# A hybrid encoder layer on one core: the MLP as seven products of 512x512x512 per block instead of eight, with its tokens in two groups of 1024

## The chip, the core and the metric

The kernel runs on one core of a Trainium2 chip. The metric is the device time of one execution in microseconds (us); lower is better. The core has TensorE (PE, matrix products into PSUM; PEld is its weight load), VectorE (DVE), ScalarE (ACT) and GpSimd (POOL) for element work, and SyncE (SP), which here issues most of the transfers; POOL issues the stores, too. Each engine runs its own instructions in order and waits on semaphores for the others. Transfers run on 16 DMA engines.

## The reference

One layer over 2048 tokens of width 1024, in float32: a projection to six parts, two kinds of mixing, an output projection, and a squared-ReLU MLP.

```python
h = rms_norm(x, norm_mix);  proj = h @ w_in                    # [2048,1024] @ [1024,3072]
na_q, na_k, na_v, r_q, r_k, r_v, r_g = split(proj)
na_out = neighbourhood_attention(na_q, na_k, na_v, rpb)        # 8 heads of 64, 32 rows x 64 columns of tokens
ret = bidirectional_retention(rotary(r_q), rotary(r_k), r_v)   # 4 heads, 16 chunks of 128, a scan over chunks
ret_out = silu(r_g) * head_group_norm(ret)
x = x + concat(na_out, ret_out) @ w_out                        # [2048,1024] @ [1024,1024]
h = rms_norm(x, norm_mlp)
x = x + square(relu(h @ w_up)) @ w_down                        # 1024 -> 4096 -> 1024
return rms_norm(x, norm_final)
```

## The kernel before, in words

**Products.** Every float32 product is three matmuls on operands that are split into a rounded part and a rest (`hi`, `lo`): hi x hi, hi x lo, lo x hi (`mm3`, L187 to L189, each 128x512). A split is one ACT cast (L175 for weights) and one DVE subtraction (L176). Weights stream from DRAM in pieces of 128 x 1024 elements (512 KB) by `ws`, with two raw buffers.

**Steps.** The main line of the program is a list of steps of 12 matmuls each. `interleave(main, fillers)` emits it, and spreads the other work (the fillers, generators with a first and a last step) between these steps. TensorE's order is this program order; what a filler's matmul waits for stops everything behind it. The steps are: projection 0 to 191 (two passes over `w_in`, for token blocks 0, 1 and then 2, 3), the output projection of block 0 192 to 207, then for each of the four blocks of 512 tokens 144 steps: 128 of the MLP (`mlp_up` and `mlp_down` alternating over eight 512-wide blocks of the hidden layer) and 16 of the next block's output projection.

**Fillers.** Neighbourhood attention runs in four groups `na(j)` of 32 tiles: two score matmuls, softmax on ACT and DVE, transposes, the product with the values (`nv`, loaded tile by tile), an add. Retention first makes its 16 chunk products (`kv`) and the `scan`; then `ret(j)` makes four chunks (`ret_chunk`, 26 yields), each with a single buffer `rg`. `na(0)` lies over steps 50 to 179 and `ret(0)` over 155 to 187; the other groups of both lie under the MLP of the block before: `na(j)` over some 107 steps, `ret(j)` over some 81. The tokens of a block stay in SBUF from the output projection to the end (`big` tiles), where the MLP's results are added to them (L979).

One retention chunk (L731 to L800) runs like this: load `rg` (L741); its exponential on ACT (L746); one add and four reciprocals on DVE (L753, L755); their product back into `rg` (L756); scores and outputs on TensorE (`rs`, `ro`, L769 to L776); statistics, the norm and the multiplication by `rg` on DVE (L780 to L789). Only after L789 is `rg` free for the next chunk's load.

## Time and profile before

| | |
|---|---|
| time, median of 3 executions | 2452.12 us (2449.55 to 2459.75) |
| the profiled execution: its span, first to last instruction | 2451.4 us |
| PE / PEld / DVE / ACT / POOL busy | 2410.5 / 1965.4 / 1396.9 / 962.0 / 176.4 us |
| mean granted TensorE clock | 0.995 of full speed |
| moved by DMA | 378.32 MB, 154 GB/s over the span |

The profiled execution is one more execution of the same kernel; its span is 0.7 us under the median of the three that were timed. "Busy" of an engine is the sum of its instructions' durations; matmuls overlap in the pipeline, and their ends are modelled, so what a matmul costs is read from the time between starts.

### The profile page before, as it was taken

Reading aid. Unit: us, or ns where it says so; the run is one execution under the profiler, and the core shown is the slowest. Engines: PE = TensorE matmul, PEld = TensorE weight load, DVE = VectorE, ACT = ScalarE, POOL = GpSimd, SP = SyncE. Lnnn points to the kernel's source line nnn. Section 1 sums busy time; section 2 is a strip of 40 time slices with the busy share of each in tenths; the row PEclk is TensorE's granted clock in tenths of the full one; section 3 lists DMA queues with packets and bytes.
Section 4 is the critical chain, followed back from the end, with each engine's and each line's share of the span. In section 5 each row is a group of like instructions: output and inputs, shape, how many; then the busy total and the mean of one; then the engine's idle time right before and its main releaser. Section 6 shows DMA issues by size and latency. Waiting matters only on the chain.

```text
span 2451.4 us, 31720 instructions
## 1 busy us (share of the span) xinstructions
PE 2410.5 (98%) x11384; PEld 1965.4 (80%) x11384; DVE 1396.9 (57%) x2810; ACT 962.0 (39%) x1690; POOL 176.4 (7%) x266
## 2 busy tenths in 40 slices
PE   7999999999999999999999999999999999999998
PEld 6888788867788887788777878888887888888886
DVE  7325354466467667545766665467666555544445
ACT  6223343323354444424544443345444423423223
POOL 1212022221100000000000000000000000000001
PEclk9999999999999999999999999999999999999999
DMA  8635566776645545543755554447554443433332
GB/s 284 185 120 171 164 200 198 239 249 188 225 136 164 155 144 157 150 134 91 226 164 146 155 156 128 129 126 213 141 156 123 119 137 96 144 101 95 95 101 71
DMA packets 238957, 378.32 MB, mean 154 GB/s; under 512 B 29009, under 2 KB 101329, under 8 KB 238801
## 3 DMA queue, kind: packets, MB, share of 16 engines
q1 hardware_dynamic: 218640, 315.46, 43.8%
q0 software_dynamic: 20160, 60.84, 7.4%
q8 instruction: 90, 1.47, 0.2%
q14 instruction: 67, 0.54, 0.1%
HBM read 313.28 MB, written 62.91 MB: 153 GB/s over the span
## 4 chain that ended last, share of the span: by engine, by line
PE 85%; DMA 6%; DVE 4%; issue 3%; ACT 2%; POOL 1%; SPq 1%; DVEq 0%; POOLq 0%; ACTq 0%
PE mm L187 26%; PE mm L189 25%; PE mm L188 25%; PE op L649 2%; PE sp L609 2%; PE tp L634 2%; DMA mraw<-d_mix 1%; DMA nv<-d_v 1%; PE sp L607 1%; PE rs L769 1%; DMA xT<-in_xT_dram 1%; PE hp L299 1%; PE ro L775 1%; DMA nql<-d_ql 1%; PE ro L776 1%
## 5 line engine op out<-in xcount | busy, mean ns | idle before, releaser
L187 PE MATMUL mm<-wh,big 128*128 128x512 f32 (+1 forms) x1784 | 700.5, 393 | 5.6 <-DVE st L440 4.7
L189 PE MATMUL mm<-wh,big 128*128 128x512 f32 (+1 forms) x1784 | 684.7, 384 | 0.5 <-DVE big L831 0.5
L188 PE MATMUL mm<-wl,big 128*128 128x512 f32 (+1 forms) x1784 | 684.3, 384 | 0.0
L176 DVE TENSOR_TENSOR wl<-raw,wh 128x1024 fp32r<-128x1024 f32 x334 | 410.6, 1229 | 449.8 <-ACT wh L175 441.6
L175 ACT CAST wh<-raw 128x1024 fp32r<-128x1024 f32 x336 | 353.2, 1051 | 720.8 <-PE mm L189 371.3
L187 PE MATMUL mm<-big,wh 128*128 128x512 f32 (+1 forms) x1376 | 545.6, 396 | 2.3 <-DVE st L440 2.3
L189 PE MATMUL mm<-big,wl 128*128 128x512 f32 (+1 forms) x1376 | 530.4, 385 | 0.0
L188 PE MATMUL mm<-big,wh 128*128 128x512 f32 (+1 forms) x1376 | 530.1, 385 | 0.0
L187 PEld LDWEIGHTS mm<-wh,big 128*128 128x128 f32 x1784 | 336.4, 189 | 79.6 <-issue 15.0
L189 PEld LDWEIGHTS mm<-wh,big 128*128 128x128 f32 x1784 | 336.5, 189 | 69.6 <-DVE big L831 1.4
L188 PEld LDWEIGHTS mm<-wl,big 128*128 128x128 f32 x1784 | 337.0, 189 | 59.8
L187 PEld LDWEIGHTS mm<-big,wh 128*128 128x128 f32 x1376 | 258.5, 188 | 61.7 <-issue 12.4
L189 PEld LDWEIGHTS mm<-big,wl 128*128 128x128 f32 x1376 | 258.5, 188 | 53.9
L188 PEld LDWEIGHTS mm<-big,wh 128*128 128x128 f32 x1376 | 259.0, 188 | 45.3
L979 DVE TENSOR_TENSOR big<-mm,big 128x512 f32<-128x512 f32 x248 | 166.6, 689 | 30.5 <-PE mm L189 29.6
L618 ACT ACTIVATE ns<-ns,nsc 128x288 f32<-128x288 f32 (+3 forms) x128 | 79.2, 618 | 230.1 <-DVE nsc L617 229.9
L612 DVE CUSTOM_DVE_ANT_0 ns<-sp,nb 128x288 f32<-128x288 f32 (+3 forms) x128 | 70.8, 553 | 97.4 <-PE sp L609 93.8
L636 ACT CAST npt<-tp 96x384 fp32r<-96x384 f32 (+3 forms) x128 | 64.3, 502 | 119.0 <-PE tp L634 118.9
L637 DVE TENSOR_TENSOR npt<-tp,npt 96x384 fp32r<-96x384 f32 (+3 forms) x128 | 74.7, 584 | 63.2 <-ACT npt L636 63.1
L940 DVE TENSOR_TENSOR st<-mm,st 128x512 f32<-128x512 f32 x128 | 87.3, 687 | 31.4 <-ACT st L939 31.0
L939 ACT ACTIVATE st<-mm 128x512 f32<-128x512 f32 x128 | 75.8, 597 | 62.5 <-PE mm L189 59.5
L620 ACT ACTIVATE ns<-ns,nsc 128x288 f32<-128x288 f32 (+3 forms) x128 | 79.2, 619 | 32.6 <-DVE nsc L619 32.3
(184 smaller groups left out, 1901.2 us busy)
## 6 DMA issues: line engine op xcount, KB each, us to landing
raw<-in_w_up_dram SPq DMA_DIRECT2D x128, 512.0 KB
raw<-in_w_down_dram SPq DMA_DIRECT2D x128, 512.0 KB
raw<-in_w_in_dram SPq DMA_DIRECT2D x48, 512.0 KB
raw<-in_w_out_dram SPq DMA_DIRECT2D x32, 512.0 KB
nv<-d_v SPq DMA_DIRECT2D x288, 36.0 KB
big<-in_x_dram SPq DMA_DIRECT2D x19, 512.0 KB
d_v<-st POOLq DMA_DIRECT2D x32, 256.0 KB, 4.9
nqh<-d_qh SPq DMA_DIRECT2D x64, 128.0 KB
```

The lines of the kernel that those rows point to most:

```text
L175: act.copy(out=hi, in_=t)
L176: (eng or dve).tensor_sub(out=lo, in0=t, in1=hi.bitcast(F32))
L187: pe.matmul(bank, lhsT=sh, rhs=mh, start=first, stop=False)
L188: pe.matmul(bank, lhsT=sh, rhs=ml, start=False, stop=False)
L189: pe.matmul(bank, lhsT=sl, rhs=mh, start=False, stop=last)
L612: dve.tensor_tensor_reduce(out=s, in0=s_ps, in1=btile[t][:, :n], scale=1.0, scalar=-3e38, op0=ALU.add, op1=ALU.max, accum_out=sc[:, 0:1])
L618: act.activation(out=s, in_=s, func=AF.Exp, bias=sc[:, 1:2], scale=1.0, accum_out=sc[:, 2:3])
L620: act.activation(out=s, in_=s, func=AF.Copy, scale=sc[:, 3:4])
L637: dve.tensor_sub(out=pt[:, :, 1], in0=t_ps, in1=pt[:, :, 0].bitcast(F32))
L939: act.activation(out=r, in_=ps, func=AF.Relu)
L940: dve.tensor_tensor(out=r, in0=ps, in1=r, op=ALU.mult)
L979: dve.tensor_tensor(out=sl, in0=ps, in1=sl, op=ALU.add)
```

## The change

The matrix work of the MLP is arranged anew. The first 1024 tokens and the second are one group each. A block of 1024 hidden columns is, for a group, a product of 1024x1024x1024; it was eight products of 512x512x512 and is now seven (Strassen's scheme in Winograd's form), for the up and for the down projection. Each product is four units of 12 matmuls: 7 x 4 x 16 = 448 units for the MLP where there were 512 steps. The scheme needs sums of quarter matrices beforehand and adds of products behind:

- up: the seven left-hand sides `S(i)` of a group's normalised tokens are made once (`prep_first_half`, `prep_rest`), split, stored to DRAM (`d_s`, 2 MB each) and loaded again for each of the four blocks, by POOL as one `wide` tile of 2 MB for each product. The sums of the weights are made on DVE from four raw quarters of 1 MB each (`Weight`).
- down: the weights' side is split to `wide` tiles on ACT and DVE, the activations' side to `narrow` tiles unit by unit; the results are added into eight `y` tiles and a shared `v`.
- The tokens between the output projection and the MLP go through DRAM (`d_y`), as do the normalised, transposed tokens (`d_hT`).
- The weights of the MLP are read twice rather than four times.
- The program falls in two stages with memory of their own. Stage 1 (224 steps): the projection in thirteen pieces (`CHUNKS`) instead of twelve pairs, the output projection of blocks 0 and 1, `na(0)` and `na(1)`, and all of retention: `kv(8, 16)` over 6 steps where it was 15, the scan over 6 where it was 10, and `ret(0)` to `ret(3)` back to back over 15 to 18 steps each. Stage 2 (480 units): 448 of the MLP and, at units 168 to 199, the output projection of blocks 2 and 3. `na(2)` and `na(3)` lie over units 10 to 164.

In the diff `quarter` loads a 128x512 piece of `d_hT`; the first list of products is that of an up block, the second that of a down block. `interleave`, `na`, `kv`, `scan` and `ret_chunk` are as before but for their buffers' pools.

```diff
-    ORDER_A = ["v", "k", "q", "rqk", "rv", "rg"]
-    ORDER_B = ["rqk", "rv", "k", "v", "q", "rg"]
+    CHUNKS = [("v", (0, 1)), ("k", (0, 1, 2)), ("q", (0, 1)), ("v", (2,)), ("rqk", (0, 1)), ("rv", (0, 1)), ("rg", (0, 1)),
+              ("rqk", (2, 3)), ("rv", (2, 3)), ("k", (3,)), ("v", (3,)), ("rg", (2, 3)), ("q", (2, 3))]
...
+    def put(g, i, kk, src):
+        turn2[0] += 1
+        o = np_.tile([P, 2, 512], F32R, tag=("n_k", "n_pt")[turn2[0] % 2], bufs=1, name=nm("so"))
+        act.copy(out=o[:, 0], in_=src)
+        dve.tensor_sub(out=o[:, 1], in0=src, in1=o[:, 0].bitcast(F32))
+        sp.dma_start(out=d_s[g][i][:, kk], in_=o.bitcast(F32))
...
+    def prep_rest(g):
+        for kk in range(4):
+            a11 = quarter(g, 0, kk, "n_qh")
+            a21 = quarter(g, 1, kk, "n_b")
+            a22 = quarter(g, 1, kk + 4, "n_v")
+            a12 = quarter(g, 0, kk + 4, "n_ql")
+            s1 = np_.tile([P, 512], F32, tag="n_t2", bufs=1, name=nm("s1"))
+            dve.tensor_tensor(out=s1, in0=a21, in1=a22, op=ALU.add)
+            dve.tensor_tensor(out=a21, in0=a11, in1=a21, op=ALU.subtract)
+            dve.tensor_tensor(out=a11, in0=s1, in1=a11, op=ALU.subtract)
+            put(g, 5, kk, a11)
+            dve.tensor_tensor(out=a12, in0=a12, in1=a11, op=ALU.subtract)
+            put(g, 6, kk, a21)
+            put(g, 3, kk, a22)
+            put(g, 4, kk, s1)
+            put(g, 2, kk, a12)
+            yield
...
+        def S(i):
+            return [lambda W: st_dma.dma_start(out=W.bitcast(F32), in_=d_s[g][i]), None, None, None]
...
+        return [
+            Product(S(0), T((0, 0)), e1, more=True),
+            Product(S(1), T((1, 0)), e2, joins=True),
+            Product(S(5), [T2(m) for m in range(4)], e6, pre=[lambda: tt(w.t[0, 0], w.t[0, 1], w.t[0, 0], SUB)]),
+            Product(S(6), T((0, 1)), e7, more=True, pre=[lambda: tt(w.t[0, 1], w.t[1, 1], w.t[0, 1], SUB)], then=ld),
...
+        return [
+            Product(T((0, 0)), S((0, 0)), shared(first_block), more=True),
+            Product(T((1, 0)), S((0, 1)), into(0, 0, "2"), joins=True),
+            Product([T3(0), None, T3(1), None], [S3(m) for m in range(4)], into(1, 1), more=True),
+            Product(T((1, 0)), S((1, 1)), into(1, 0), joins=True, then=ld),
+            Product(T((0, 1)), S((0, 0)), shared(None), pre=[sums], then=ld),
+            Product(T((0, 0)), S((1, 0)), into(1, 1, "5"), more=True, then=ld),
+            Product(T((1, 1)), S((0, 1)), into(0, 1, "3"), joins=True, then=ld),
...
-                (unlend(("g", "st", "kT", "qxT")), 1, 134, 134), (scan(), 17, 145, 154),
-                (ret(0), RET_STEPS, 155, 187),
-                (na(0), NA_STEPS, 50, 179),
-            fill.append((ret(j), RET_STEPS, m - 6, m + 75))
+                (unlend(("g", "st", "kT", "qxT")), 1, 150, 150), (scan(), 17, 151, 156),
+                (na(1), NA_STEPS, 112, 183),
+                (ret(0), RET_STEPS, 157, 171), (ret(1), RET_STEPS, 172, 188),
+                (ret(2), RET_STEPS, 189, 204), (ret(3), RET_STEPS, 205, 222),
+                (late(lambda: norm_in(0)), 5, 210, 215), (late(lambda: prep_first_half(0)), 4, 216, 221)]
         interleave(main, fill)
+        first.close()
...
+        fill = [(late(lambda: norm_in(1)), 5, 2, 5), (late(lambda: prep_rest(0)), 4, 6, 6),
+                (late(lambda: na(2)), NA_STEPS, 10, (o0 - 6) // 2), (late(lambda: na(3)), NA_STEPS, (o0 - 6) // 2 + 1, o0 - 4),
...
+        interleave(run_products(prods), fill)
```

Three places show how instructions move. The first is SP's queue between two loads of `rg`, where the weight loads (`raw`) mark how many main steps lie between. Before, inside the MLP of block 0, these are the last rows ahead of the load of `rg_7492` (`nv`, `nk`, `nqh` and `nb` are attention's loads, `rst`, `rqk`, `rqx` and `rv` retention's); the load of `rg` before that one stands sixteen rows above them, with five more weight pieces on the way.

```order
L163 DMA raw_7201<-in_w_down_dram 128x2x512
L574 DMA nk_7211<-d_kl 64x1024
L577 DMA nqh_7214<-d_qh 64x512
L631 DMA nv_7264<-d_v 32x4x128 x2
L163 DMA raw_7262<-in_w_down_dram 128x2x512
L631 DMA nv_7264<-d_v 32x4x128 x2
L737 DMA rqx_7487<-d_rqT 64x4x128 x2
L596 DMA nb_7317<-in_bias_dram 128x512
L163 DMA raw_7309<-in_w_down_dram 128x2x512
L631 DMA nv_7401<-d_v 24x3x128 x5
L739 DMA rv_7490<-d_rv 128x512
L163 DMA raw_7399<-in_w_up_dram 128x2x512
```

The same queue now, from one chunk of `ret(2)` to the next (`mraw` belongs to the output projection).

```order
L743 DMA rg_7746<-d_rg 128x512
L762 DMA rst_7797<-d_st 64x512
L763 DMA rst_7797<-d_st 64x512
L739 DMA rqx_7926<-d_rqT 64x4x128 x2
L168 DMA raw_7768<-in_w_out_dram 128x2x512
L832 DMA mraw_7771<-d_mix 128x2x512
L741 DMA rv_7929<-d_rv 128x512
L168 DMA raw_7837<-in_w_out_dram 128x2x512
L743 DMA rg_7931<-d_rg 128x512
```

Before, nine weight pieces lay between two chunks, and now two: a piece serves two steps, so some 18 steps have become four. The second place is POOL's queue where stage 2 begins: the last output projection's stores (`d_y`), the first two `wide` loads (`d_s_95` and `d_s_96` are `S(0)` and `S(1)`), the second half of the normalised tokens, and the `wide` load of the third product (`d_s_100` is `S(5)`).

```order
L856 DMA d_y<-st_8423 128x512
L1056 DMA wide_8747<-d_s_95 128x4096
L1056 DMA wide_8758<-d_s_96 128x4096
L890 DMA d_hT<-hev_8842 128x4x128
...
L890 DMA d_hT<-hev_8961 128x4x128
L1056 DMA wide_9122<-d_s_100 128x4096
L1056 DMA wide_9124<-d_s_101 128x4096
```

SP's queue between the last of those `d_hT` stores and that `wide` load holds the loads of quarters (`sq`) and the stores of `put` (`so`); here are its last third and the end.

```order
L904 DMA d_s_100<-so_9062 128x1024
L904 DMA d_s_101<-so_9067 128x1024
L908 DMA sq_9083<-d_hT 128x512
L908 DMA sq_9085<-d_hT 128x512
L904 DMA d_s_98<-so_9071 128x1024
L904 DMA d_s_99<-so_9075 128x1024
L908 DMA sq_9087<-d_hT 128x512
L904 DMA d_s_97<-so_9079 128x1024
L908 DMA sq_9089<-d_hT 128x512
L904 DMA d_s_100<-so_9095 128x1024
```

Nothing of this stood in the program before: the sixteenth `put` of `prep_rest` is the last piece of `d_s_100`, and the third product of the first up block starts only behind its load. The third place is DVE's queue in a down block. Before (block 7 of the last group), two weight splits stand behind four adds into the tokens:

```order
L979 TENSOR_TENSOR big_3365_17611<-mm_19742,big_3365_17611 128x512
L979 TENSOR_TENSOR big_3365_17611<-mm_19743,big_3365_17611 128x512
L979 TENSOR_TENSOR big_3365_17611<-mm_19744,big_3365_17611 128x512
L979 TENSOR_TENSOR big_3365_17611<-mm_19745,big_3365_17611 128x512
L176 TENSOR_TENSOR wl_19805<-raw_19740,wh_19804 128x1024
L176 TENSOR_TENSOR wl_19839<-raw_19774,wh_19838 128x1024
```

Now (the first product of a down block in group 1, four units; L1165 is the add into `v`, L1018 a `narrow` split, L1023 a `wide` split, L1131 and L1132 sums of weights):

```order
L1165 TENSOR_TENSOR v_17135<-mm_19242,v_17135 128x512
L1132 TENSOR_TENSOR wq_19078<-wq_19078,wq_19161 128x1024
L1018 TENSOR_TENSOR narrow_19268<-ff_18876,narrow_19268 128x4x128
L1023 TENSOR_TENSOR wide_19246<-t_3525_19289,wide_19246 128x2x512
L1165 TENSOR_TENSOR v_17135<-mm_19267,v_17135 128x512
L1018 TENSOR_TENSOR narrow_19285<-ff_18876,narrow_19285 128x4x128
L1131 TENSOR_TENSOR wq_19161<-wq_19240,wq_19002 128x1024
L1165 TENSOR_TENSOR v_17135<-mm_19284,v_17135 128x512
L1132 TENSOR_TENSOR wq_19078<-wq_19078,wq_19161 128x1024
L1018 TENSOR_TENSOR narrow_19309<-ff_18876,narrow_19309 128x4x128
L1165 TENSOR_TENSOR v_17135<-mm_19308,v_17135 128x512
```

Where a product took an add for each accumulator and half a weight split for each step, it takes, unit by unit, an add, a `narrow` split and one 128x1024 operation.

## Rows read from the trace of the kernel before

**Rows 1.** The page: busy time of the engines, and the chain that ended last.

```profile
PE 2410.5 (98%) x11384; PEld 1965.4 (80%) x11384; DVE 1396.9 (57%) x2810; ACT 962.0 (39%) x1690; POOL 176.4 (7%) x266
PE 85%; DMA 6%; DVE 4%; issue 3%; ACT 2%; POOL 1%; SPq 1%; DVEq 0%; POOLq 0%; ACTq 0%
```

**Rows 2.** Stretches: start:end, length, busy us (x count), clock, DMA share, GB/s.

```profile
481.00:530.00 49.00, 44.27 (x184) 34.48 (x183) 27.79 (x83) 13.30 (x31) 11.89 (x22) 0.90 0.86 279
700.00:1130.00 430.00, 429.67 (x2094) 350.97 (x2093) 268.63 (x537) 182.55 (x318) 7.39 (x12) 1.00 0.50 146
2200.00:2428.00 228.00, 228.00 (x1008) 188.79 (x1007) 104.67 (x125) 64.97 (x82) 0.00 (x0) 1.00 0.30 91
2428.00:2451.40 23.40, 11.63 (x52) 9.29 (x50) 14.13 (x44) 9.41 (x23) 10.17 (x8) 0.79 0.24 90
```

**Rows 3.** Timeline of TensorE in a quiet stretch: start, duration, instruction; first and tenth.

```profile
2299.84 0.39 PE L189 MATMUL mm<-big,wl 128*128 128x512 f32 x1
...
2301.88 0.39 PE L189 MATMUL mm<-big,wl 128*128 128x512 f32 x1
```

**Rows 4.** Timelines of TensorE, DVE, SP and ACT: one retention chunk into the next.

```profile
545.71 0.38 PE L775 MATMUL ro<-rv,ra 128*128 128x128 f32 x2
...
547.70 0.49 DVE L780 BATCH_NORM_STATS2 rbs<-ro 128x6 f32<-128x128 f32 x2 [4.31 <-PE ro L776]
...
553.77 0.69 DVE L789 TENSOR_TENSOR rst<-rst,rg 128x512 f32<-128x512 f32 x1
...
554.49 0.34 SPq L741 DMA_DIRECT2D rg<-d_rg  x1
...
557.24 0.63 ACT L746 ACTIVATE ra<-rg 128x512 f32<-128x512 f32 x1 [0.42 <-DMA rg<-d_rg]
...
558.36 3.39 DVE L755 RECIPROCAL ra<-ra 128x128 f32<-128x128 f32 x4
561.78 0.69 DVE L756 TENSOR_TENSOR rg<-rg,ra 128x512 f32<-128x512 f32 x1
```

**Rows 5.** Stretches round two TensorE waits in the scan, columns as in Rows 2.

```profile
504.00:506.30 2.30, 0.34 (x2) 0.00 (x0) 1.83 (x6) 0.00 (x0) 1.32 (x3) 1.00 0.86 248
506.30:516.60 10.30, 7.52 (x17) 5.44 (x18) 6.18 (x21) 3.73 (x10) 5.53 (x11) 0.50 0.98 341
516.60:530.00 13.40, 13.40 (x62) 10.72 (x62) 8.09 (x14) 4.44 (x8) 0.00 (x0) 1.00 0.75 235
```

**Rows 6.** DMA issues: KB each, and the median us from issue to landing.

```profile
d_v<-st POOLq DMA_DIRECT2D x32, 256.0 KB, 4.9
...
out_dram<-big POOLq DMA_DIRECT2D x12, 512.0 KB, 4.2
...
d_kv<-ra POOLq DMA_DIRECT2D x16, 256.0 KB, 4.1
```

**Rows 7.** Groups of DVE instructions: count, busy us, mean ns of one, idle before.

```profile
L176 DVE TENSOR_TENSOR wl<-raw,wh 128x1024 fp32r<-128x1024 f32 x334 | 410.6, 1229 | 449.8 <-ACT wh L175 441.6 <-DMA nv<-d_v 6.1 <-DMA nk<-d_kh 1.1
L979 DVE TENSOR_TENSOR big<-mm,big 128x512 f32<-128x512 f32 x248 | 166.6, 689 | 30.5 <-PE mm L189 29.6
...
L637 DVE TENSOR_TENSOR npt<-tp,npt 96x384 fp32r<-96x384 f32 (+3 forms) x128 | 74.7, 584 | 63.2 <-ACT npt L636 63.1
L612 DVE CUSTOM_DVE_ANT_0 ns<-sp,nb 128x288 f32<-128x288 f32 (+3 forms) x128 | 70.8, 553 | 97.4 <-PE sp L609 93.8 <-DMA nb<-in_bias_dram 3.3
...
L652 DVE TENSOR_TENSOR nt<-op,not 128x128 f32<-128x128 f32 x128 | 36.4, 284 | 45.4 <-ACT not L651 45.1
...
L657 DVE TENSOR_TENSOR nmx<-nmx,nt 64x512 f32<-64x512 f32 x32 | 21.9, 683 | 18.3 <-ACT nmx L656 18.2
...
L619 DVE RECIPROCAL nsc<-nsc 128x1 f32<-128x1 f32 x128 | 20.3, 159 | 46.8 <-ACT ns L618 46.5
```

**Rows 8.** Waits of TensorE for a DMA: us in total, times, longest.

```profile
PE op L649 <- DMA nv<-d_v: 3.2, 3, 2.1
```

**Rows 9.** The page: DMA queues SP (q1) and POOL (q0): packets, MB, share.

```profile
q1 hardware_dynamic: 218640, 315.46, 43.8%
q0 software_dynamic: 20160, 60.84, 7.4%
```

More of the change, by code (lines that the diff above doesn't have):

```diff
@@ L103, in trunk @@
     d_mix = dp.tile([1024, SEQ], F32, name="d_mix")
+    d_y = dp.tile([SEQ, D], F32, name="d_y")
+    d_hT = dp.tile([D, SEQ], F32, name="d_hT")
+    d_s = [[dp.tile([P, 4, 2, 512], F32, name=f"d_s{g}{i}") for i in range(7)] for g in range(2)]
     uid = [0]
@@ L1086, in trunk, with chain, once, late @@
+        return {"2": lambda m: half(m, 0), "6": a6, "5": lambda m: half(4 + m, 1), "3": lambda m: half(m, 1)}
     hTs = {}
     res = {}
-    groups = [Group(j) for j in range(NG)]
+    def chain(*gens):
+        for g in gens:
+            yield from g
+    def once(fn, *a):
+        fn(*a)
+        yield
+    def late(fn):
+        yield from fn()
     with tc.manual_schedule(engines={mybir.EngineType.PE}):
@@ L1153, in late @@
[L1153 to L1161 removed]
+        mixes = {0: [], 1: []}
+        OUT = 8 * sum(len(b) for _, b in CHUNKS)
```

692 lines of the change are left out of this document (412 added, 280 removed).

## The prediction

> **What bounds the kernel now.** I read the page first: TensorE is busy for 2410.5 of 2451.4 us, DVE for 57%, ACT for 39%, and the chain that ended last is 85% TensorE [rows 1]. Then stretches, to see whether that holds everywhere. In a stretch with attention and retention in it TensorE is busy for 429.67 of 430 us, with DVE at 268.63 (62%); in a stretch of nothing but the MLP 228.00 of 228, with DVE at 104.67 (46%) [rows 2]. TensorE waits at the edges only: 4.7 us round the scan (44.27 of 49), about 12 in the tail [rows 2]. So the kernel is bound by the number of matmuls, and whatever removes matmuls is paid in full as long as the others keep up. How far they are from not keeping up is what decides here.
>
> **What is removed.** The MLP takes 512 steps of 12 matmuls, 6144 in all, and will take 448 units, 5376: 768 full matmuls less. In a quiet stretch ten starts lie 2.04 us apart, nine intervals of 0.227 us [rows 3]. 768 x 0.227 = **174 us saved**. A step is 12 x 0.227 = 2.72 us. All else on TensorE stays: projections, attention, retention, transposes.
>
> **What is added, stage 1.** The scan: the second eight `kv` chunks now have 6 steps instead of 15. A chunk needs a load (2.75 us from issue to use for 256 KB [rows 4]), half a microsecond or so on DVE twice, its matmuls and a copy, some 5 us in a single-buffered loop, and the steps now offer 3.3 us with its own matmuls: 8 x 1.7 = 14. The scan itself may add 6. Against that, the 4.7 us of waits and the half clock which stood there before (10.3 us at 0.50 [rows 5]) are partly the same waits: about 10 of them are gone or counted twice. **+10** (0 to 25).
>
> Retention: its chunks ran far apart and now run back to back. A chunk's loop through the single `rg` is, in the trace: outputs 545.71 to the first statistic 547.70, 2.0; statistics, Newton steps and norm to the end of L789 at 554.46, 6.8; load, exponential, add, four reciprocals and product, 554.49 to 562.47, 8.0 [rows 4]; the two score masks on DVE 0.7 more. That is 17.5 us. The four groups get 15, 17, 16 and 18 steps, 4.1 a chunk, 11.2 us; the chunk's own matmuls add about 3 (2.0 for the outputs, half of that for the rest, an estimate) and attention about 1 in the first two groups. TensorE thus offers 15 us and the loop asks for 17.5 and, since DVE's weight splits (1.23 us [rows 7]) now fall among its small operations, rather 18: 3 x 16 = **+45** (25 with the loop at 17 and the steps stretched by other fillers; 80 with the loop at 20).
>
> **The change of stage.** The memory of stage 2 comes free when stage 1's last matmul is done. The last stores of tokens must land (4.1 to 4.9 us [rows 6]) before SP's load of them goes out, and behind that in SP's queue stand the first weight quarters; beside them POOL loads two `wide` tiles. Until the first unit can start 3 to 8 MB must land, at 341 GB/s (what the full queues moved in the scan [rows 5]) 9 to 23 us, and a split follows. I take **+16** (10 to 22).
>
> **The hole at the third product.** Units 0 to 7 are covered by `S(0)` and `S(1)`, made in stage 1. The third product needs `S(5)`, and its last piece is the sixteenth `put` of `prep_rest(0)`, which can start only when the transposes between units 2 and 5 have been stored to `d_hT` (4 to 5 us) and loaded (2.75). A `put` is a cast of 0.63, a subtraction of 0.69, an issue of 0.34 to 0.5 and a 512 KB store of 4.2 us [rows 4, 6, 7] until its buffer is free, 6 us; there are two buffers, so 3 us for each: 16 x 3 = 48. Then the 2 MB `wide` load, 6 us at 341 GB/s and some 2 to land. Sum 4.5 + 2.75 + 2 + 48 + 8 = 65, of which units 6 and 7 hide 5. TensorE has nothing else: attention begins at unit 10 and its matmuls stand behind. **+60** (45, if the stores land faster when little else moves, to 80).
>
> **Half clock.** After waits of 3 us and 2 us the granted clock went to 0.50 for 10.3 us; at 516.6 it was back at 1.00 [rows 5]. Three longer holes (change of stage, third product, one in the scan) cost half of such a stretch each: **+8**, of which the retention stretch may want more (0 to 20).
>
> **The down blocks.** Per block of 28 units, 76.2 us of matmuls, DVE does 28 operations of 128x1024 (14 `wide` splits, 8 sums of weights, 6 of activations) and 60 of 128x512 (28 adds, 28 `narrow` splits, 4 sums): at 1.229 and 0.689 [rows 7] 75.8 us, 99% where it was 46%. With independent operations in a row I expect some 10% less. The three blocks that share their time with attention get more: five of its groups are 224 us of DVE in all, 56 for each of its four groups [rows 7]; two groups over 155 units make 20 us a block, so 96. Attention's own matmuls bring some 100 into a block, at most 0.227 each; take 16. DVE 96 against TensorE 92: with every unit waiting for its `narrow` split a queue that is this full will miss now and then. 5 us for each of three blocks, **+15** (0 to 40), and nothing for the five without attention (0 to 30). The up blocks need 4 and 56, 43.5 us, and are free.
>
> **Attention under `wide` loads.** Attention's steps run at 1.35 to 1.7 for each unit where they were 0.75 to 0.9, so a tile has some 6 to 7.5 us for its chain of load, transposes and products, which I put at 5. Its value loads made TensorE wait 3.2 us in all before [rows 8]. 56 `wide` loads of 2 MB, 6 us each at 341 GB/s, now run beside them from POOL's queue, which carried 60.84 MB in all before [rows 9]. **+10** (0 to 40). The Trainium skill, "DMA: Bandwidth & Descriptors", section "Issuing engines are not separate DMA queues", says that transfers issued by SP and by POOL run on the same 16 engines and interleave. By that rule a value load beside a `wide` load takes longer, for about half of the tiles; at 2.5 us more each the slack would just be used up, and the sum would be the same, but at 4 us more it would be 1.5 x 64 = 96 higher. No row here shows a 2 MB transfer beside attention.
>
> **Sum.** From the profiled span, 2451.4 (0.7 below the median of the timed runs): - 174 + 10 + 45 + 16 + 60 + 8 + 15 + 10 = 2441.4. The tail holds eight more GpSimd products, ahead of the last accumulators, and I leave it equal (-8 to +8). The terms for waits overlap in part (a wait for retention hides one for attention, a half clock is within a wait), which I put at -8: **2433 us**, 0.8% less. Terms at their lower ends give 2451 - 174 + 80 = 2357, at their upper ends 2451 - 174 + 345 = 2622; several upper ends at once are unlikely.
>
> **Rivals.**
> *The waits are mostly covered.* If retention's chunks overlap better than the loop says (the exponential and the load of the next chunk moved ahead of the statistics) and `put` stores land in 2.5 us, retention costs 15 and the hole 35: 2433 - 30 - 25 = 2378, and down to 2340 with the other terms low. For it: DVE and ACT have room in stage 1 (57% and 39% over the span). Against it: the loop is a chain of dependences, not a matter of load.
> *The retention loop decides, and the kernel is slower.* Place: the 16 chunks over steps 157 to 222. Price: each microsecond of a chunk's period beyond 15 costs 16 us. At 18 it is in the sum; it takes 2433 + 31 to be slower by 0.5%, so from 20 us on. At 23 (DVE splits, adds and attention of `na(1)` between each two steps of the chain, the loads of `rg` behind waiting weight loads on SP) it is 2433 + 80 = 2513. For it: in the trace a chunk shares SP's queue with loads that wait for buffers, and it never had fewer than 8 steps, 22 us. Against it: nothing in the loop is longer than the reciprocals' 3.39 us [rows 4].
> *DVE becomes the bound of all eight down blocks.* At 12 us for each, 96 instead of 15: 2514. For it: 99% by means. Against it: up blocks between them have half of DVE free.
> *Shared DMA engines*, as above: 2433 + 60 = 2493 with half of that price.
>
> **How the numbers follow.** What a measurement of this kernel can tell from no change is about 0.5%, 12 us. The forecast as it stands has 0.42 (its own range 2400 to 2470: faster 0.27, same 0.11, slower 0.04); covered waits 0.22, all faster; retention 0.20, slower; DVE 0.10 (slower 0.08, same 0.02); DMA 0.06 (slower 0.03, same 0.03). Faster 0.49, same 0.16, slower 0.35. The range reaches from the middle of the covered case to the retention rival and DVE's with a little more: 2345 to 2530.
>
> **What would show it.** Right: 768 full matmuls fewer at the same 0.227; TensorE idle about 60 us ahead of the third product, with SP storing `d_s` all the while; chunks of retention 18 us apart with TensorE waiting for DVE (`ra`, `rst`) and for `rs`; DVE over 85% in down blocks without holes on TensorE; one gap of 16 us between the stages. Wrong: a chunk period of 15 or of over 20, a hole under 35, waits on `narrow` in the down blocks of group 1, or a cadence above 0.23 in the quiet blocks.

## The result, and the profile after

The changed kernel takes 2757.94 us (median of 4, 2747.79 to 2763.97) where the kernel before takes 2453.02 beside it: ratio 1.1233, interval 1.1204 to 1.1263. It is 12% slower; forecast were 2433 us and, at the most, 2530.

The page of the changed kernel, the lines that answer to [rows 1] and [rows 9]:

```profile
PE 2352.1 (85%) x10520; PEld 1897.5 (69%) x10520; DVE 1717.4 (62%) x3358; ACT 1139.4 (41%) x2126; POOL 257.4 (9%) x390
PE 47%; issue 22%; DMA 15%; DVE 10%; POOL 3%; ACT 2%; SPq 2%; POOLq 0%; DVEq 0%; ACTq 0%
q1 hardware_dynamic: 204336, 305.50, 35.8%
q0 software_dynamic: 32768, 192.97, 19.5%
```

The span is 2754.0 us. 864 matmuls are gone, 192 of them half as wide, which is worth the 768 full ones of the forecast, 174 us. But TensorE's busy time fell by 58 only, and its idle time rose from 40.9 us (2451.4 - 2410.5) to 401.9. So 361 us of waits came, and some 116 us (174 - 58) in which the matmuls that are left ran longer: - 174 + 361 + 116 = 303, the difference of the spans. The second is the clock, granted at 0.924 on the mean where it was 0.995: by the trace's clock records 236 us of TensorE's busy time lie in stretches at the lower of its two levels (0.50, that is 1.2 of 2.4 GHz), where it was 11, and half of the difference is 113 of the 116. The chain of waits, 85% TensorE before, is 47% TensorE. SP's queue carries about what it did, POOL's 192.97 MB instead of 60.84, most of it the 56 `wide` loads.

Where the time is lost stands in the stretches of the changed kernel (columns as in [rows 2]: start:end, length, busy of PE, PEld, DVE, ACT and POOL, clock, DMA share, GB/s):

```profile
0.00:200.00 200.00, 179.61 (x774) 145.56 (x775) 91.72 (x216) 74.78 (x126) 35.84 (x62) 0.98 0.62 204
200.00:640.00 440.00, 376.40 (x1843) 306.38 (x1843) 178.87 (x447) 168.21 (x351) 72.01 (x99) 0.91 0.55 158
640.00:700.00 60.00, 33.94 (x140) 26.44 (x139) 35.67 (x102) 15.64 (x33) 13.96 (x26) 0.79 0.80 259
700.00:1085.00 385.00, 300.70 (x1367) 241.39 (x1367) 248.03 (x673) 107.05 (x229) 39.87 (x65) 0.86 0.56 176
1085.00:1140.00 55.00, 27.57 (x118) 22.19 (x117) 24.72 (x45) 11.94 (x24) 7.83 (x14) 0.72 0.86 319
1140.00:1250.00 110.00, 35.47 (x134) 26.90 (x133) 41.87 (x73) 25.73 (x46) 4.13 (x7) 0.64 0.70 239
1250.00:1340.00 90.00, 80.86 (x363) 62.91 (x363) 69.63 (x129) 58.27 (x112) 1.09 (x2) 0.96 0.54 156
1340.00:1700.00 360.00, 324.59 (x1433) 254.12 (x1432) 232.38 (x474) 179.67 (x366) 13.10 (x24) 0.96 0.58 181
1700.00:1880.00 180.00, 178.95 (x817) 144.46 (x816) 140.45 (x246) 104.76 (x193) 8.01 (x14) 1.00 0.46 148
1880.00:2100.00 220.00, 177.28 (x754) 142.21 (x753) 154.77 (x231) 88.69 (x153) 18.70 (x29) 0.91 0.72 252
2100.00:2700.00 600.00, 599.99 (x2645) 495.94 (x2645) 454.11 (x620) 279.98 (x447) 26.01 (x40) 1.00 0.45 162
2700.00:2754.00 54.00, 36.75 (x152) 28.99 (x150) 45.19 (x110) 24.71 (x50) 16.82 (x12) 0.87 0.21 78
```

Length less PE's busy time is the idle time of each. The stretches are, in order: the start; the projection with `na(0)`, `na(1)` and the `kv` chunks (63.6 us idle, of it 12.1 in `kv` waiting for its load of `rv`); the scan, with attention beside it (26.1, of it 9.8 and 12.6 in two products of attention, the first behind the scan's operations on DVE); retention (84.3); the change of stage (27.4); the hole at the third product (74.5); attention in stage 2 (9.1 and 35.4); its last tiles, to 1797.1, and the output projection (1.1); the start of group 1 (42.7); and 600 us of up and down blocks in which TensorE is never idle.

What TensorE waited for in the whole run (total us, times, longest; the row that answers to [rows 8] is the second):

```profile
PE mm L1000 <- DMA wide<-d_s: 66.0, 1, 66.0
PE op L651 <- DMA nv<-d_v: 54.0, 17, 12.6
PE ry L796 <- DVE rst L791: 43.8, 10, 11.7
PE sp L609 <- DMA nqh<-d_qh: 29.7, 10, 7.6
PE mm L1000 <- ACT narrow L1017: 24.8, 3, 22.6
PE hp L886 <- DVE xn L877: 23.2, 2, 18.4
```

The cadence is what it was in [rows 3]: in a quiet stretch the first and the tenth start are again 2.04 us apart.

```profile
2598.81 0.39 PE L1000 MATMUL mm<-wide,narrow 128*128 128x512 f32 x1
...
2600.85 0.39 PE L1000 MATMUL mm<-wide,narrow 128*128 128x512 f32 x1
```

The sixteen loads of `rg` (SP; durations min/median/max in ns, then first and last start) stand (1064.3 - 684.8) / 15 = 25.3 us apart, where 18 was forecast:

```profile
L743 SPq DMA_DIRECT2D rg<-d_rg x16: 319/335/532, 684.8 to 1064.3; - x16
```

One such chunk, from load to load, in the timelines of TensorE, DVE, ACT and SP (this answers to [rows 4]; in brackets the idle time before a row and what ended it):

```profile
929.60 0.32 SPq L743 DMA_DIRECT2D rg<-d_rg  x1
...
933.31 1.76 DVE L757 RECIPROCAL ra<-ra 128x128 f32<-128x128 f32 x2
...
936.28 2.74 DVE L855 TENSOR_TENSOR st<-mm,st 128x512 f32<-128x512 f32 x4 [1.21 <-PE mm L194]
...
938.94 1.76 DVE L757 RECIPROCAL ra<-ra 128x128 f32<-128x128 f32 x2
...
940.61 1.16 DVE L181 TENSOR_TENSOR wl<-raw,wh 128x1024 fp32r<-128x1024 f32 x1
...
942.40 0.76 DVE L772 TENSOR_TENSOR ra<-rs,dmat 128x256 f32<-128x256 f32 x2
942.93 0.77 PE L777 MATMUL ro<-rv,ra 128*128 128x128 f32 x2 [4.63 <-issue]
...
946.72 0.30 DVE L782 BATCH_NORM_STATS2 rbs<-ro 128x6 f32<-128x128 f32 x1 [3.56 <-PE ro L778]
...
948.79 1.23 DVE L834 TENSOR_TENSOR big<-mraw,big 128x1024 fp32r<-128x1024 f32 x1 [1.77 <-ACT big L833]
...
956.13 0.68 DVE L791 TENSOR_TENSOR rst<-rst,rg 128x512 f32<-128x512 f32 x1
...
956.85 0.34 SPq L743 DMA_DIRECT2D rg<-d_rg  x1
956.96 0.63 PE L796 MATMUL ry<-ident,rst 128*128 128x128 f32 x4 [3.88 <-DVE rst L791]
```

Read it as a conversation of two queues. DVE's row of reciprocals, four in one piece before, is cut by the output projection's adds (L855), which had themselves waited 1.21 us for TensorE; a weight split follows; then TensorE, which has stood for 4.63 us (the row names no releaser; the mask L772, which its product needs, stands behind all this on DVE), makes the outputs (from the first of them to the first statistic 3.8 us, 942.93 to 946.72, where [rows 4] has 2.0: half clock); then DVE stands behind L834, a split that waits for ACT; and `ry` waits 3.88 us for L791. Each engine does other work in its own order and arrives late at the next link.

### The profile page after: what moved, and what is told of

Same layout as the page of the kernel before. It is cut to its first block, busy times and chain, and to the rows that moved or that the text cites. A ratio compares the mean times of both kernels' runs of the same rounds, so it can differ in the third digit from the quotient of the medians.

```text
span 2754.0 us, 31380 instructions
## 1 busy us (share of the span) xinstructions
PE 2352.1 (85%) x10520; PEld 1897.5 (69%) x10520; DVE 1717.4 (62%) x3358; ACT 1139.4 (41%) x2126; POOL 257.4 (9%) x390
## 3 DMA queue, kind: packets, MB, share of 16 engines
q0 software_dynamic: 32768, 192.97, 19.5%
## 4 chain that ended last, share of the span: by engine, by line
PE 47%; issue 22%; DMA 15%; DVE 10%; POOL 3%; ACT 2%; SPq 2%; POOLq 0%; DVEq 0%; ACTq 0%
PE mm L1000 11%; PE mm L1002 11%; PE mm L1001 11%; DMA nv<-d_v 3%; PE mm L192 3%; PE mm L193 3%; PE mm L194 3%; DMA d_s<-so 2%; DMA nql<-d_ql 1%; PE op L651 1%; DVE narrow L1018 1%; PE sp L611 1%; DMA sq<-d_hT 1%; DMA mraw<-d_mix 1%; DVE wide L1023 1%
## 5 line engine op out<-in xcount | busy, mean ns | idle before, releaser
L1000 PE MATMUL mm<-wide,narrow 128*128 128x512 f32 x1920 | 772.4, 402 | 92.7 <-DMA wide<-d_s 66.0
L1002 PE MATMUL mm<-wide,narrow 128*128 128x512 f32 x1920 | 761.5, 397 | 22.1 <-DVE narrow L1018 22.0
L1001 PE MATMUL mm<-wide,narrow 128*128 128x512 f32 x1920 | 759.1, 395 | 0.0
L1000 PEld LDWEIGHTS mm<-wide,narrow 128*128 128x128 f32 x1920 | 368.0, 192 | 176.5 <-issue 74.7
L1002 PEld LDWEIGHTS mm<-wide,narrow 128*128 128x128 f32 x1920 | 367.1, 191 | 107.2 <-DVE narrow L1018 28.3
L1001 PEld LDWEIGHTS mm<-wide,narrow 128*128 128x128 f32 x1920 | 368.0, 192 | 72.6
L192 PE MATMUL mm<-wh,big 128*128 128x512 f32 (+1 forms) x632 | 259.6, 411 | 0.2 <-DVE st L441 0.2
L193 PE MATMUL mm<-wl,big 128*128 128x512 f32 (+1 forms) x632 | 248.4, 393 | 0.0
L194 PE MATMUL mm<-wh,big 128*128 128x512 f32 (+1 forms) x632 | 247.3, 391 | 0.0
L192 PEld LDWEIGHTS mm<-wh,big 128*128 128x128 f32 x632 | 130.7, 207 | 26.7 <-issue 3.3
L194 PEld LDWEIGHTS mm<-wh,big 128*128 128x128 f32 x632 | 129.2, 204 | 24.4
L193 PEld LDWEIGHTS mm<-wl,big 128*128 128x128 f32 x632 | 130.5, 206 | 20.8
L1023 DVE TENSOR_TENSOR wide<-wq,wide 128x1024 fp32r<-128x1024 f32 x112 | 136.5, 1228 | 10.2 <-ACT wide L1022 9.9
L192 PE MATMUL mm<-big,wh 128*128 128x512 f32 x320 | 135.6, 424 | 2.8 <-DVE st L427 2.0
L1018 DVE TENSOR_TENSOR narrow<-wq,narrow 128x512 fp32r<-128x512 f32 x192 | 131.7, 687 | 8.5 <-ACT narrow L1017 8.0
L1018 DVE TENSOR_TENSOR narrow<-ff,narrow 128x512 fp32r<-128x512 f32 x192 | 133.6, 697 | 1.3 <-ACT narrow L1017 0.9
```

What stands on the lines that cost most here:

```text
L192: pe.matmul(bank, lhsT=sh, rhs=mh, start=first, stop=False)
L193: pe.matmul(bank, lhsT=sh, rhs=ml, start=False, stop=False)
L194: pe.matmul(bank, lhsT=sl, rhs=mh, start=False, stop=last)
L1000: pe.matmul(banks[m], lhsT=sh, rhs=mh, start=first_, stop=False, skip_group_check=True)
L1001: pe.matmul(banks[m], lhsT=sh, rhs=ml, start=False, stop=False, skip_group_check=True)
L1002: pe.matmul(banks[m], lhsT=sl, rhs=mh, start=False, stop=last_, skip_group_check=True)
```

## The experiments

Busy and idle time of TensorE are from the page of each run (idle is the span less busy).

**Pace alone, in the kernel before.** Two runs give the kernel before about the changed kernel's density of fillers, one filler each, and change nothing else. First retention, each group over 16 steps:

```diff
-                (ret(0), RET_STEPS, 155, 187),
+                (ret(0), RET_STEPS, 155, 170),
...
-            fill.append((ret(j), RET_STEPS, m - 6, m + 75))
+            fill.append((ret(j), RET_STEPS, m - 6, m + 9))
```

> The kernel before with one thing moved: each group of four retention chunks gets 16 steps instead of 33 or 82, as in the changed kernel; everything else is as before. Theory (the pace is the cause: a chunk is a chain through VectorE, one load and TensorE's program order, about 25 us long in the changed kernel's trace, and TensorE has about 15 us of other work for it): some 10 us lost for each of 16 chunks, 2451 + 120 to 170 = 2570 to 2620, with TensorE waiting at ry and ro. Rival (the loss belongs to the changed kernel's first stage, where output projection, norm and transfers crowd VectorE and the queues): under 60 us more, below 2510.

Measured: 2582.59 us, ratio 1.0524 (1.0499 to 1.0548), 131 us more with not one instruction more. Idle went from 40.9 to 127.3 us, busy from 2410.5 to 2452.5; within a group the chunks' `ry` lie 19 to 29 us apart. The wait named first is the changed kernel's:

```profile
PE ry L794 <- DVE rst L789: 46.6, 14, 7.2
PE ro L775 <- DVE ra L770: 10.5, 4, 4.4
```

Second, attention, over 56 to 72 steps a group instead of 108 to 130:

```diff
-                (na(0), NA_STEPS, 50, 179),
+                (na(0), NA_STEPS, 50, 105),
...
-            fill.append((na1, NA_STEPS - 5, 201, m + 100) if j == 1 else (na(j), NA_STEPS, m - 7, m + 100))
+            fill.append((na1, NA_STEPS - 5, 201, m + 64) if j == 1 else (na(j), NA_STEPS, m - 7, m + 64))
```

> The kernel before with attention compressed as in the changed kernel: group 0 over 56 steps instead of 130, the others over some 70 instead of some 107. Theory (pace): single-buffered loads of values and queries cannot follow, TensorE waits for nv and nqh; the changed kernel lost about 150 us over its attention stretches beyond what it lost before, so 2451 + 80 to 150 = 2530 to 2600. Rival (the 2 MB loads and the weight quarters of the changed kernel hold attention's loads up): under 30 us more.

Measured: 2599.59 us, ratio 1.0593 (1.0567 to 1.062), 148 us more; idle 142.8, busy 2460.1.

```profile
PE op L649 <- DMA nv<-d_v: 37.3, 15, 6.2
PE sp L607 <- DMA nqh<-d_qh: 10.8, 7, 3.4
```

So the two fillers, each pressed together by itself, cost 131 and 148 us, added up more than the 174 that the scheme saves, before any of its own work is counted; and attention needs no `wide` load beside it to wait for its values. The idle time, too, is that of the changed kernel: 86 us more with retention pressed (84 in its stretch there), 102 more with attention (94 there, in both stages).

**Leaving a filler out of the changed kernel.** Without the sixteen retention chunks:

```diff
-                (ret(0), RET_STEPS, 157, 171), (ret(1), RET_STEPS, 172, 188),
...
-                (ret(2), RET_STEPS, 189, 204), (ret(3), RET_STEPS, 205, 222),
```

> The changed kernel without the sixteen retention chunks of steps 157 to 222 (the output projections read attention's rows twice instead); chunk products and scan stay. Chunks' own matmuls are some 50 us. Theory (the dense chunks cost 150 us beyond their matmuls): 2754 - 50 - 120 to 160 = 2545 to 2585. Rival (the stretch is slow for its norm, output projection and transfers as well, so the waits stay): above 2640.

Measured: 2584.39 us, ratio 1.0527 (1.049 to 1.0564), 174 us less than the changed kernel (1.1233). Idle fell by 75 us (401.9 to 326.9), busy by 95 (2352.1 to 2257.0), and the waits of the rest stand as they did (`wide` 62.1, `nv` 47.4, `nqh` 31.0). Of the 95 us, TensorE's busy time at half clock (236 us in the changed kernel, 171 here) explains about 33; so the chunks' own matmuls are about 62, and 108 of the 170 by which the spans differ are what dense retention cost beyond them, less than the 120 to 160 expected. Without `na(2)` and `na(3)`:

```diff
-                (late(lambda: na(2)), NA_STEPS, 10, (o0 - 6) // 2), (late(lambda: na(3)), NA_STEPS, (o0 - 6) // 2 + 1, o0 - 4),
```

> The changed kernel without attention groups 2 and 3, which lie over units 10 to 164 (the output projection reads groups 0 and 1 in their place). Their matmuls are some 88 us, the waits in their stretch some 60 to 75. Theory (pace of attention): 2754 - 88 - 60 to 75 = 2590 to 2606, and the down blocks in that stretch run without a wait. Rival (the stretch waits for VectorE, which the down blocks fill by themselves): only the matmuls and half of that go, 2625 to 2650.

Measured: 2579.32 us, ratio 1.0507 (1.047 to 1.0543), somewhat under what was expected: idle 351.2, busy 2227.1. The stretches in which attention stood, 1250 to 1700 before, are now without a gap, with `wide` loads and DVE at 81% in the first of them:

```profile
1250.00:1340.00 90.00, 90.00 (x399) 74.55 (x398) 73.06 (x95) 43.47 (x67) 1.06 (x2) 1.00 0.33 111
1340.00:1650.00 310.00, 310.00 (x1370) 256.76 (x1369) 230.20 (x305) 141.13 (x219) 6.34 (x12) 1.00 0.43 151
```

The products themselves run without loss; what they run beside does not.

**Mending links.** For the last eight retention chunks a second buffer for `rg`, a buffer of its own for the normed output, and `ry` behind the next chunk's score masks:

```diff
-        sg = rt("g", [P, RH, P])
+        late_ = n >= 8
+        sg = np_.tile([P, RH, P], F32, tag="n_t2", bufs=1, name=nm("rg")) if late_ and n % 2 else rt("g", [P, RH, P])
...
+        if prev:
+            prev.pop()()
...
+        yn = np_.tile([P, RH, P], F32, tag="n_mx", bufs=1, name=nm("ry")) if late_ else rt("st", [P, RH, P])
```

> The changed kernel with the chain cut in the last eight retention chunks: a second buffer for rg, so that load and exponential no longer wait for the norm of the chunk before, a buffer of its own for the normed result, and the transposes ry put behind the score masks. Theory (chain with TensorE's order): period of these chunks from 25 down to 17 to 20, 8 x 5 to 8 = 40 to 65 us less, 2695 to 2715. Rival (VectorE or transfers are simply full there): less than 15 us gained.

Measured: 2733.92 us, ratio 1.1142 (1.1111 to 1.1173), 24 us less, under what was expected. From the eighth chunk's load of `rg` to the sixteenth's it is 188 us where it was 214. Between them lie 8 to 40 us, three times 16 to 19, the last two, in `ret(3)`, 31; and `ry` still waited for DVE, 21.2 us in 5. There DVE's queue also holds the norm and the preparation that stage 2 needs. Buffers and order, which this run doesn't separate, loosen the loop through `rg`; they don't take the foreign work out of DVE's row.

A second buffer for `nv` in `na(2)` and `na(3)`:

```diff
-            vt = np_.tile([P, 4, P], F32R, tag="n_v", bufs=1, name=nm("nv"))
+            if j >= 2 and t % 2:
+                vt = cp.tile([P, 4, P], F32R, tag="xn", bufs=2, name=nm("nv"))
+            else:
+                vt = np_.tile([P, 4, P], F32R, tag="n_v", bufs=1, name=nm("nv"))
```

> The changed kernel with a second buffer for the values of attention in groups 2 and 3. Theory (one buffer from the product of a tile to the load of the next): waits for nv in stage 2 (17 us, and what follows each) go, 20 to 40 us less, 2714 to 2734. Rival (the queue of SP, which issues four or five transfers of 0.43 us for a tile behind a bias load that waits for VectorE): under 10 us.

Measured: 2732.75 us, ratio 1.1135 (1.1102 to 1.1167), 25 us less; `nv` 54.0 to 30.0 us in all. In that half the product waits for `nv` no more (23.4 us before), and more for `nqh` (20.8 us where it was 13.0): the single buffer was the wait there, and part of it went to the next one.

The hole: `prep_rest` in the order in which the products need its results, `S(5)` first, at the price of more loads.

```diff
+        for kk in range(4):
+            a11 = quarter(g, 0, kk, ("n_qh", "n_ql")[kk % 2])
+            a21 = quarter(g, 1, kk, ("n_b", "n_t2")[kk % 2])
+            a22 = quarter(g, 1, kk + 4, "n_v")
+            dve.tensor_tensor(out=a22, in0=a21, in1=a22, op=ALU.add)
+            dve.tensor_tensor(out=a11, in0=a22, in1=a11, op=ALU.subtract)
+            put(g, 5, kk, a11)
+        yield
...
```

> The changed kernel with the sums of the up projection made in the order in which the products want them: all four pieces of S(5) first, then S(6), S(3), S(4), S(2), at the price of more loads of quarters. Theory (the hole at the third product is the sixteen stores through two buffers): the wait of 66 us falls to about 35, with some 5 to 10 given back ahead of the next products: 20 to 30 us less, about 2730. Rival (it is the landing of d_hT and the queue ahead of it): no change.

Measured: 2807.04 us, ratio 1.144 (1.1412 to 1.1467), 49 us more where 20 to 30 less were expected. The hole did shrink from 66.0 to 38.9 us ("wide<-d_s", one wait), but attention's `nk`, whose buffer the puts use too, had been waiting under its cover:

```profile
PE sp L609 <- DMA nk<-d_kl: 73.9, 2, 71.8
```

The same with `na(2)` from unit 32 on:

> As a_put5, with attention group 2 begun at unit 32 instead of 10, so that its first key load no longer stands behind the stores of prep_rest (the two share buffers). Theory: the wait of 72 us at the first score goes, the one at the third product stays near 39: 2807 - 60 to 75 plus 5 to 15 for the denser attention = 2740 to 2760, about as the changed kernel or a little less. Rival (the stores hold up the products themselves): still above 2780.

Measured: 2815.5 us, ratio 1.1468 (1.1437 to 1.15), no gain either: the wait for `nk` is gone, and the hole is back in pieces ("wide<-d_s", 84.8 us in 5, the longest 35.6). A product takes four units, 10.9 us, and needs four puts; its puts of `S(5)` left SP about 5 us apart (stores at 1149.1, 1154.1, 1159.3 and 1164.5), so these come to 20. The hole is the throughput of that chain. In the changed kernel's order, with fewer loads, sixteen puts left SP 3.0 us apart (1151.09 to 1195.51), so the new order also made the chain slower; what an order without more loads would give was not tried.

**The scheme for half of the tokens, with the fillers at their old pace.** The hybrid is the kernel before through the MLP of block 1, and takes seven products for the second 1024 tokens alone. That saves half, 384 matmuls, 87 us. Attention has 82 to 89 steps a group, retention 77 to 80, and the last two output projections, norms and preparations lie under block 1's MLP.

```diff
-        for g in range(2):
+        for g in (1,):
...
+    SEQ_1 += [("d", 5), ("o", 2), ("o", 3), ("u", 6), ("u", 7), ("d", 6), ("d", 7)]
...
+        fill += [(na1, NA_STEPS - 5, 201, 282), (na(2), NA_STEPS, 283, 370), (na(3), NA_STEPS, 371, 459),
+                 (ret(1), RET_STEPS, 202, 278), (ret(2), RET_STEPS, 279, 356), (ret(3), RET_STEPS, 357, 436),
```

> The kernel before up to the MLP of block 1, then the seven products for the second group of 1024 tokens alone. Attention and retention keep room: groups 1 to 3 of attention over 82 to 89 main steps each instead of some 107, retention over 77 to 80 instead of 82; the output projections of blocks 2 and 3 come 16 steps ahead of the end of block 1's MLP, the sums S are made under those steps, and the normalised result of block 1 is stored before the memory changes hands. Theory (the seven products pay in full where nothing else has to keep up; the losses of the changed kernel are the pace of what lies beside them): 384 matmuls less, 87 us; change of stage 15 to 30, denser attention 5 to 20, rest of the hole 0 to 20: 2390 to 2440, below the kernel before. Rival (the change of stage and the making of the sums cost as much again as in the changed kernel): 2460 or more.

Measured: 2506.44 us, ratio 1.021 (1.0188 to 1.0232), no gain, as the rival had it. From 700 to 1500 us TensorE is idle for 35 us, and from 1500 to 1900, the norms, puts and the change of stage, for 68; behind them not at all:

```profile
700.00:1500.00 800.00, 764.93 (x3661) 609.86 (x3660) 524.62 (x1201) 366.94 (x706) 20.09 (x33) 0.98 0.56 155
1500.00:1900.00 400.00, 332.45 (x1462) 266.67 (x1461) 220.31 (x396) 144.18 (x259) 29.29 (x47) 0.91 0.68 228
1900.00:2450.00 550.00, 550.00 (x2429) 455.40 (x2428) 406.95 (x537) 256.38 (x405) 19.71 (x28) 1.00 0.41 148
```

The same with block 1's result stored by ACT instead of POOL (`(act if g.j else st_dma).dma_start(out=out[...])`):

> As hybrid, with the last four stores of block 1 issued by ScalarE instead of GpSimd, so that the first two 2 MB loads do not stand behind them in GpSimd's queue. Theory: 5 to 12 us less than hybrid. Rival (the memory of those loads comes free no earlier, or ScalarE's casts wait instead): the same within 5.

Measured: 2501.17 us, ratio 1.0209 (1.0183 to 1.0236), the same: the wait at the change of stage moved from `wide` (30.3 us) to `narrow` (37.2).

Then two steps: attention at 92 steps a group and retention at 83, the projections 16 steps later, five put buffers (`hybrid2`); and that with a second `nv` buffer (`hybrid3`).

> As hybrid_act, with three things: output projections of blocks 2 and 3 sixteen steps later, so that attention's groups have 92 steps each again nearer to the 107 of before; five buffers for put instead of two, its stores issued by GpSimd; the final gain for block 1 loaded ahead of prep_rest. Theory: the 30 us at the change of stage in hybrid were loads standing behind put's stores in SP's queue, and fall to 10 to 15; attention's excess falls by 10 to 20; 2501 - 15 to 20 - 10 to 20 = 2461 to 2476, or less if put no longer stops ScalarE and VectorE (9 us). Rival (the stores move the same wait to GpSimd's queue, and the hole at the third product comes back with 10 to 30): 2485 or more.

> As hybrid2, with a second buffer for attention's values, for one staging buffer less (five instead of six). Theory (a single buffer is what the denser attention waits for): 10 to 20 us less than hybrid2. Rival (the staging buffers of projections and MLP are then short): the same or more.

Measured: 2497.36 us, 1.0171 (1.0157 to 1.0185), and 2485.16 us, 1.0114 (1.0097 to 1.0131). The first missed what was expected, the second met it. What attention gave back reappeared in one wait of 50 us for the first `narrow` of the stage. Next, the order of the queues there (puts back on SP, first weights by POOL):

> The previous hybrid (seven products for the second 1024 tokens alone, second value buffer) lost 51.5 us in one wait of TensorE for the first narrow split after the change of stage. Changed here: the put stores are back on SP; the square's scratch tile of block 1's norm leaves the buffer that SP's last gain load shared; the first weight quarters go on POOL's queue, in turn with the wide loads; the last two norms and preparations are spread further apart. Theory (queue order: the first weights stood behind a blocked load and behind 6 MB of wide loads): that wait falls to 12-25 us and the time by 30 to 45, to 2440-2455, which equals the kernel before. Rival (it is the bytes: weights and wide tiles of the first products must all land and the queues are full): the wait stays over 40 or moves to the third product, and the time stays at 2475 or more.

Measured: 2502.11 us, 1.0206 (1.0187 to 1.0226). The wait grew to 78.8 us, and the time stayed where the rival had it, but not for its reason. What the first `narrow` split of ACT waited for last is neither weights nor bytes of the next stage, but a store of block 1's result:

```profile
1867.19 2.18 ACT L1256 CAST narrow<-wq 128x512 fp32r<-128x512 f32 x4 [19.08 <-DMA out_dram<-big]
```

I read it so: the `narrow` tiles lie where block 1's tokens lay, and these go out only behind the norm's squares, which stand behind the puts in ACT's queue. So the last run does two things at once: it puts four `y` tiles there, and it ends the preparation earlier, which gives attention 86 steps a group again:

```diff
-    SEQ_1 += [("d", 6), ("o", 2), ("o", 3), ("u", 7), ("d", 7)]
+    SEQ_1 += [("d", 5), ("o", 2), ("o", 3), ("u", 6), ("u", 7), ("d", 6), ("d", 7)]
...
+        accs[1].y = {t: bp.tile([P, D], F32, tag=f"y{t}", bufs=1, name=nm("y")) for t in range(4)}
         mats[0][3].load(1, st_dma)
```

> In the previous hybrid the first narrow split waited 78.8 us, until 1867, although its weights had landed: it waited for the stores of block 1's result (its tile lay where block 1's tokens had lain), and those for the norm's squares on ScalarE, which stood behind the puts of the second half of the preparation. Neither the order of the weight loads nor the bytes: the end of stage 1's own work. Changed here: the output projections of blocks 2 and 3 stand two products earlier (attention at 86 steps a group instead of 92, retention at 78 instead of 83), so that the preparation ends 15 steps before the stage does; and the first four y tiles, which are not needed until later, are laid where block 1's tokens lay, so that narrow does not wait for them. Theory: the wait at the change of stage falls from 79 to 15-30 us, attention gives back 0 to 20; 2502 - 55 to - 75 + 0 to 20: 2430 to 2465. Rival (the stage change costs what the bytes cost: 7 MB of weights and wide tiles at once): the wait stays over 45 or appears again at the third product, time 2475 or more.

Measured: 2463.97 us, ratio 1.0046 (1.0029 to 1.0063). The wait for `narrow` is 11.6 us, the hole at the third product 2.4:

```profile
PE mm L193 <- DVE big L986: 13.5, 5, 4.5
PE mm L1239 <- ACT narrow L1256: 12.8, 2, 11.6
PE mm L1239 <- DMA wide<-d_s: 2.4, 1, 2.4
```

Most of the long wait at the change of stage was thus no cost of the scheme as such; which of the two edits took it away was not separated. This is the best version found, and it is 0.5% slower than the kernel before: 87 us saved, 104 lost (the spans are 2468.6 and 2451.4). Of that TensorE is idle for 23 us from 700 to 1500, where attention has 86 steps a group, and for 38 from 1700 to 1860: 13.5 for adds (`big` L986) that stand in DVE's queue behind puts which wait for their loads, 11.6 for `narrow`, 8.4 for the transposes' `xn`. None found beats the kernel before.

## Why the prediction was wrong

The account runs from the forecast's 2433 to the span of 2754, 321 us. Each row is a term of the sum, beside the idle time of its stretch beyond that of the kernel before.

| term of the sum | put | measured | off by |
|---|---|---|---|
| matmuls removed | - 174 | - 174 | 0 |
| `kv` and scan | 10 | 33 (12.1 + 26.1 - 4.7) | 23 |
| retention | 45 | 84, idle alone | 39 |
| attention in stage 1 | 0 | 48 (63.6 - 12.1 - 3.8) | 48 |
| change of stage | 16 | 27 | 11 |
| hole at the third product | 60 | 75, with what lies about it | 15 |
| attention in stage 2 | 10 | 46 (9.1 + 35.4 + 1.1) | 36 |
| down blocks beside attention | 15 | 0 (from 1250 to 1880 TensorE waits at attention's matmuls only) | - 15 |
| start of group 1 | 0 | 43 | 43 |
| half clock | 8 | 116, everywhere | 108 |
| overlap, start, tail, small waits before | - 8 | 5 | 13 |

Three sums are off in themselves, and none of them decides: 3 x 16 is 48 where 45 is put; three halves of 10.3 us are 15 where the half clock is put at 8; and half of 96 us is 48, which gives the rival of the shared DMA engines 2481 and not 2493.

**What was right.** The gain is paid in full where the products run alone: 600 us without a gap, at the old cadence. The hole is what its sum said, 66.0 us against 65 less what two units hide, with the puts 3.0 us apart as the sum had them. POOL's queue shows it: the `wide` load of `S(5)` stood idle for the last put's store.

```profile
1198.77 0.55 POOL L1056 DMA_DIRECT2D wide<-d_s  x1 [56.15 <-DMA d_s<-so]
```

**The retention term failed by its loop.** "That is 17.5 us", 18 with splits among it, took the links of [rows 4] as they stood in a chunk with room around it. At 25.3 the rival "the retention loop decides" (at 23, 2513) had the mechanism and nearly the pace, with 0.20. Not only the loop's own links count: what DVE does between them waits for TensorE, and TensorE, in program order, waits for the next link; the run with retention alone pressed together (19 to 29 us a chunk, 131 us) shows it without any of the other changes.

**The attention term was the worst step.** It was priced only by whether `wide` loads would disturb it, and so only in stage 2. "Some 6 to 7.5 us for its chain of load, transposes and products, which I put at 5" sets a mean time beside a sum for which it shows no row. And in stage 1 no price was put at all, though the 1.35 to 1.7 steps a unit that the term names are those of `na(1)` and `na(0)` there (97 steps over 72 and over 56); the groups of stage 2 have 1.26 (97 over 77). Both stages lose alike, and in stage 1 no `wide` load runs. There the wait for `nv`, from 200 to 640, is the first row here, and in stage 2, from 1250 to 1700, the second:

```profile
PE op L651 <- DMA nv<-d_v: 17.9, 8, 5.7
...
PE op L651 <- DMA nv<-d_v: 23.4, 8, 6.0
```

The same number of waits, nearly of the same length, 14 `wide` loads or none: by this the loads have no price. Shorter stretches of stage 2 say otherwise. The second and the fourth row are those in which the 14 loads run (up blocks); in the others none is issued:

```profile
1250.00:1370.00 120.00, 109.97 (x497) 85.44 (x496) 93.70 (x177) 75.77 (x146) 1.62 (x3) 0.97 0.55 159
1370.00:1500.00 130.00, 103.60 (x445) 80.42 (x445) 64.19 (x141) 53.39 (x112) 5.73 (x11) 0.93 0.60 190
1500.00:1597.00 97.00, 95.38 (x436) 75.19 (x436) 85.72 (x157) 62.11 (x120) 1.37 (x3) 0.99 0.42 122
1597.00:1697.00 100.00, 93.51 (x412) 73.64 (x411) 57.44 (x126) 44.63 (x98) 5.47 (x10) 0.96 0.68 228
1697.00:1800.00 103.00, 101.95 (x462) 80.68 (x462) 90.39 (x170) 67.77 (x132) 1.61 (x3) 0.99 0.45 139
```

With the loads TensorE is idle for 32.9 of 230 us, without for 12.7 of 320, though DVE is fuller there; and of the product's eight waits for `nv` seven, 22.9 of the 23.4 us, lie in the two stretches with the loads. This agrees with the rule of the Trainium skill, "DMA: Bandwidth & Descriptors", section "Issuing engines are not separate DMA queues", that transfers of both queues run on the same 16 engines and interleave. It is not shown that the loads are the cause, since up and down blocks differ in other work too and no run changed the loads alone. What is shown is that the loss doesn't need them: attention pressed together in the kernel before, where no such load exists, cost 148 us. And with a second `nv` buffer the product no longer waits for `nv` in stage 2, with the 14 loads still there (25 us back).

**The half clock was the largest miss.** The term took three long holes. But some 110 waits, two thirds of them of 1 to 12 us, are spread over the fillers' stretches (about 50 between 420 and 1085), and the granted clock stood at 0.86 to 0.96 on the mean of the retention and attention stretches, 0.64 to 0.79 about the long holes, a mixture of its full and its half level, while in 2100 to 2700 it is 1.00. [Rows 5] had shown that two waits of 2 and 3 us cost 10 us at half clock; that is a price for each cluster of short waits, not for each long hole, and the term counted no clusters. That the clock follows the waits is seen in both dense runs (86 and 102 us more of idle time came with 42 and 50 more of busy time, at the same instructions); it could not be varied by itself.

**The down blocks were overrated.** 99% DVE by means gave a term and a rival of 0.10. DVE comes to 49.06 of 50 us in a window of group 1's down blocks, and TensorE loses nothing. Part of it is that the durations overlap: three operations of 0.69 us start at 2200.26, 2200.87 and 2201.47, 0.60 apart, so that durations added up overstate what DVE needs.

```profile
2200.00:2250.00 50.00, 49.99 (x219) 40.52 (x219) 49.06 (x62) 27.48 (x42) 0.00 (x0) 1.00 0.24 76
```

**Left out altogether:** the start of group 1 (42.7 us, of it 18.4 in one wait of the transposes for `xn` and 19.3 in seven for `narrow`), where output projection, norm, puts and loads follow one another once more as at the change of stage. It was not tried by itself.

## What to carry to other kernels

Work that costs an in-order engine nothing as a filler has a price in pace: before steps are taken away from under a chain of small operations, press that chain together in the old kernel and measure; here this alone cost 131 and 148 us against a gain of 174. Load by means says little either way: independent work ran at 98% of DVE without a gap, and a chain of dependences over DVE, TensorE and ACT left TensorE idle for 22% of its stretch with DVE at 64%. And price a wait with the clock that follows it: of 477 us lost, 116 were matmuls that ran slower, nearly all of it at half clock between and after the waits.
